# A hybrid SSD and DeltaNet step on one core: x loaded in 2 KB pieces from two queues, the first norm's sums of squares halved between two engines, two small loads held back

## The chip, the cores and the metric

The kernel runs on one core of one Trainium2 chip. The metric is the device time of one execution in microseconds (us), lower is better. Before the change it was 2331.97 us, the median of three runs (2331.62 to 2332.45).

## The reference, cut to what matters

The reference is one inference step of one layer. 336 tokens (16 learned meta tokens and 256 prompt tokens form one stream, 64 sample tokens the other) of width 2048 are normalised by their root mean square, and everything else follows from that normalised input:

```
xf = x * lax.rsqrt(jnp.mean(x * x, axis=-1, keepdims=True) + EPS)
u  = xf * norm_mix_w
z_a, xbc_a, dt_a, qkv_b, z_b, beta_b, a_b, gate_a, gate_b = split(u @ w_in)
...                              # branch A: conv, SiLU, chunked SSD scan, gated group norm
ya = ya + xs * ssd_d             # ssd_d: one number for each of 32 heads
...                              # branch B: conv, L2 norms, chunked gated delta rule
mix = sigmoid(gate_a) * (ya @ w_out[:2048]) + sigmoid(gate_b) * (ob @ w_out[2048:])
h = x + mix
h = h + square(relu(rmsnorm(h) @ w_up)) @ w_down
```

All inputs and outputs are float32. The weights w_in, w_out, w_up and w_down are large (some 340 MB are read from HBM in a run); x itself is 2.75 MB.

## The kernel before, in words

Activations are kept transposed: features on the 128 partitions, 336 tokens along the row. Each float32 product is made of three matmuls: an operand is split into a rounded high part and a low rest (`hi`, `lo` for weights, `uh`, `ul` for the normalised input), and the kernel adds hi x uh, hi x ul and lo x uh. PE is TensorE, ACT ScalarE, DVE VectorE, POOL GpSimd, and SP the engine that issues nearly all loads and stores.

**The weight stream.** Weights come in chunks `raw` of 512 KB, in a fixed order, numbered here from 0. `wload(n)` (L198) issues the load of chunk n; there are three buffers, so the load of chunk n waits until the split of chunk n - 3 has read its buffer. `wsplit(n)` writes `hi` on ACT (L61) and `lo` on DVE (L64; for chunk 3 on POOL). A projection of 256 columns (`pbig`, L58) takes four chunks, 24 matmuls each. Chunks 0 to 3 are the first projection, made while `uh` and `ul` are still being written; chunks 4 to 7 are the second.

**The start (L288 to L379).** x lies in three tiles x0, x1, x2 of 112 tokens on the partitions and 2048 features in a row. For each tile there is a sum of squares (`sumsq`, into `ssx`), a root (`root`: scale and add on DVE, power on POOL, into `rsx`), and 16 transposes on PE in four groups (`flip`, into a PSUM tile `pu`), copied to `xT`. The roots are laid on a diagonal (`spread_d`, `dgx`) and multiplied by a matrix of ones (`prx`), so that each partition holds the root of every token (`rbx`). Before the transposes PE multiplies the identity eight times (`pwarm`).

**The splits of u (L380 to L387 and the loop at L460).** `u_scale(k)` multiplies a feature block of `xT` by `rbx` (`ut`, even k on DVE, odd k on POOL); `u_split(k)` writes `uh` on ACT and `ul` on DVE. Six matmuls of the first projection follow each of the 16 blocks.

**Behind it.** Small parameters are loaded (L476 to L504) into `cra`, `crb`, `sra`, `srb`, `pb`, `wt` and `dvec`; `nega` is computed from `pb` on ACT and stands in ACT's queue between two `uh`; `wt` is split (`wtr`) and multiplied with u (`ptok`, 32 matmuls), from which per-token numbers are computed (`tok`, `la`) and summed on PE (`pcum`). `dvec` holds `ssd_d` and is first used much later. `xT` is stored to DRAM (`xTd`, L999, 16 stores) and four scratch tensors there are filled with zeros (`aD`, `uD`, L1004, 12 stores), all for later use.

**What sets the order.** PE runs in the order of the program text. Inside a `manual_schedule()` block (L342 to L472) all engines do; outside it, a scheduler with its own time estimates orders the other engines, SP's queue among them. Each DMA issued takes the next of eight completion semaphores, and waits until the DMA that had it before has landed. An engine runs its queue in order, and SP is an engine in this sense: an issue that waits holds up all behind it. The tile pool of x is given back after the last transpose (`xctx.close()`), and `cra` and its neighbours lie in that memory.

Of the kernel before, what the change touches and what calls it, by code (L numbers as in the profile page):

```python
# [8 lines left out]
F32 = mybir.dt.float32  # L9
F32R = mybir.dt.float32r  # L10
AF = mybir.ActivationFunctionType
ALU = mybir.AluOpType
# [3 lines left out]
D = 2048  # L16
KD = D // P
# [7 lines left out]
EPS = 1e-6  # L25
# [17 lines left out]
def tile_hybrid_step(ctx: ExitStack, tc: tile.TileContext, i: dict, o: dict):  # L43
    nc = tc.nc
# [9 lines left out]
    def scr(name):  # L54
        return pss.tile([P, 512], F32, tag="sc", name=name)

    def mm(out, lhsT, rhs, start=True, stop=True, **kw):
        nc.tensor.matmul(out, lhsT=lhsT, rhs=rhs, start=start, stop=stop, **kw)  # L58

    def act(out, in_, func=AF.Copy, **kw):  # L60
        nc.scalar.activation(out=out, in_=in_, func=func, **kw)  # L61

    def tt(eng, out, a, b, op):
        eng.tensor_tensor(out=out, in0=a, in1=b, op=op)  # L64
# [4 lines left out]
    V, G = nc.vector, nc.gpsimd  # L69
    MUL, ADD, SUB = ALU.mult, ALU.add, ALU.subtract  # L70
# [5 lines left out]
    ident = const.tile([P, P], F32, name="ident")  # L76
    make_identity(nc, ident)
    ones = const.tile([P, P], F32, name="ones")
# [6 lines left out]
    def transp(out, in_):  # L85
        n = in_.shape[0]
        nc.tensor.transpose(out, in_, ident[:n, :n])
# [10 lines left out]
    def new_u(name):  # L98
        return (keep.tile([P, KD, NT], F32R, tag="uh", name=name + "h"),
                keep.tile([P, KD, NT], F32R, tag="ul", name=name + "l"))  # L100

    uh, ul = new_u("u")
    acc = keep.tile([P, KD, NO], F32, name="acc")

    par = const.tile([P, 73], F32, name="par")
# [4 lines left out]
    dvec = const.tile([P, 16], F32, name="dvec")  # L110
# [82 lines left out]
    def wload(n):  # L193
        if n >= len(stream) or n in raws:
            return
        raw = wpool.tile([P, 4, 256], F32, tag="raw", name="raw", bufs=3)
        for c0, src in stream[n]:
            nc.sync.dma_start(raw[:, :, c0:c0 + src.shape[1]], src.rearrange("(k p) c -> p k c", p=P))  # L198
        raws[n] = raw

    def wsplit(n):
        if n >= len(stream) or n in split:
            return
        wload(n)
        hi = wpool.tile([P, 4, 256], F32R, tag="hi", name="hi", bufs=3)
        act(hi, raws[n])
        lo = wpool.tile([P, 4, 256], F32R, tag="lo", name="lo", bufs=3)
        tt(G if n == 3 else V, lo, raws[n], hi.bitcast(F32), SUB)
        split[n] = hi, lo
# [62 lines left out]
    sp0 = start.enter_context(tc.tile_pool(name="sp0", bufs=1))  # L272
# [3 lines left out]
    zero = sp0.tile([P, 4 * DG // P], F32, name="zero")  # L276
# [11 lines left out]
    xs = []  # L288
    segs = [[(0, "meta", 0, 16), (16, "pr", 0, 96)], [(0, "pr", 96, 112)], [(0, "pr", 208, 48), (48, "sa", 0, 64)]]
    src = {"meta": i["meta_tokens"], "pr": i["x_prompt"][0], "sa": i["x_sample"][0]}  # L290
    def load_x(n):
        for p0, s, r0, nr in segs[n]:
            nc.sync.dma_start(xs[n][p0:p0 + nr, :], src[s][r0:r0 + nr, :])

    for n in range(3):
        xs.append(xp.tile([112, D], F32, name=f"x{n}"))
    load_x(0)
    load_x(1)
    prow = sp0.tile([73, P], F32, name="prow")
    for r0, name, nr in ((NM, "norm_mix_w", 16), (SN, "ssd_norm_w", 16), (NP_, "norm_mlp_w", 16), (CB_, "ssd_conv_b", 24), (GN, "gdn_norm_w", 1)):  # L300
        nc.sync.dma_start(prow[r0:r0 + nr, :], i[name][0].rearrange("(t c) -> t c", c=P))
    load_x(2)
    warm = sp0.tile([P, 1], F32, name="warm")
    act(warm, ones[:, 0:1], AF.Square)

    def load_cols(dst, row, n):
        ps = scr("pcol")
        transp(ps[:, :n], row[:n, :])
        V.tensor_copy(dst, ps[:, :n])
# [2 lines left out]
    xT = [cpool.tile([P, 4, NT], F32, tag=t, name="xT", bufs=b) for t, b in (("q", 2), ("k", 2), ("v", 1))]  # L312
    xT.append(sp0.tile([P, 4, NT], F32, name="xT3"))
    junk = acc.rearrange("p k n -> p (k n)")[:112, :]
    ssx = sp0.tile([112, 4], F32, name="ssx")
    rsx = sp0.tile([112, 3], F32, name="rsx")
    dgx = sp0.tile([112, 3, 112], F32, name="dgx")
    rbx = sp0.tile([P, NT], F32, name="rbx")
    HD = D // 2

    def sumsq(f, x, d0, n):
        d = junk[:, d0:d0 + x.shape[1]]
        if f is act:
            act(d, x, AF.Square, accum_out=ssx[:, n:n + 1])
        else:
            V.scalar_tensor_tensor(out=d, in0=x, scalar=1.0, in1=x, op0=MUL, op1=MUL, accum_out=ssx[:, n:n + 1])

    def flip(n, k):
        ps = scr("pu").rearrange("p (k t) -> p k t", k=4)[:, :, :112]
        for m in range(4):  # L330
            transp(ps[:, m, :], xs[n][:, (k + m) * P:(k + m + 1) * P])
        return xT[k // 4][:, :, n * 112:(n + 1) * 112], ps

    def root(n):
        r = rsx[:, n:n + 1]
        V.tensor_scalar(out=r, in0=ssx[:, n:n + 1], scalar1=1.0 / D, scalar2=EPS, op0=MUL, op1=ADD)
        tt(G, r, r, nhalf_pow[:112, 0:1], ALU.pow)

    def spread_d(n):
        V.tensor_scalar(out=dgx[:, n, :], in0=ident[:112, :112], scalar1=rsx[:, n:n + 1], scalar2=None, op0=MUL)  # L340

    manual = ExitStack()  # L342
    manual.enter_context(tc.manual_schedule())

    pw_ = scr("pwarm")
    for n in range(8):
        mm(pw_[:, :P], ident, ident)
    prx = psb.tile([P, 512], F32, tag="big", name="prx")
    sumsq(act, xs[0], 0, 0)
    for k in range(0, KD, 4):  # L350
        (V.tensor_copy if k < 8 else act)(*flip(0, k))
    root(0)
    sumsq(V, xs[1], D, 1)
    for k in range(0, KD, 4):
        act(*flip(1, k))
    root(1)
    load_cols(par, prow, 73)
    for n in range(3):
        wload(n)
    sumsq(act, xs[2][:, :HD], 0, 2)  # L360
    sumsq(V, xs[2][:, HD:], D, 3)
    tt(V, ssx[:, 2:3], ssx[:, 2:3], ssx[:, 3:4], ADD)
    root(2)
    spread_d(0)
    spread_d(1)
    act(*flip(2, 0))
    late = [flip(2, k) for k in (4, 8, 12)]
    spread_d(2)
    wsplit(0)
    for n in range(3):  # L370
        mm(prx[:, n * 112:(n + 1) * 112], ones[:112, :], dgx[:, n, :])
    act(rbx, prx[:, :NT])
    for a in late:
        act(*a)
    xctx.close()
    sp = start.enter_context(tc.tile_pool(name="sp", bufs=1))
# [107 lines left out]
    srb_src = i["state_gdn_conv"][0, 0].rearrange("k (t c) -> (k t) c", c=P)  # L484
    for n in range(2):
        nc.sync.dma_start(srb[n], srb_src[n * 72:(n + 1) * 72, :])
    for h in range(2):
        nc.sync.dma_start(dvec[h * 64:(h + 1) * 64, :], i["ssd_d"][0].rearrange("(t h) -> h t", h=2)[h].partition_broadcast(64))
    pb = sp.tile([P, 2, 48], F32, name="pb")
# [16 lines left out]
    for n in range(2):  # L506
        w, wr = wt[:, n * 8:(n + 1) * 8, :], wpool.tile([P, 8, P], F32R, tag="hi", name="wtr", bufs=3)
# [697 lines left out]
    with tc.manual_schedule():  # L1205
        for t in range(3):
            final_part(7, t)
            r, n = frs[:, t:t + 1], toks[t][1]
            stt(r[n], fss[n, t, 7:8], 1.0 / D, fsum[n, t:t + 1], MUL, ADD)
            tt(G, r[n], r[n], nhalf_pow[n, 0:1], ALU.pow)  # L1210
        for m in range(2):
            for t, (_, n, t0) in enumerate(toks):
                dst = o["y_prompt"][0, t0:t0 + P, :] if t < 2 else o["y_sample"][0]
                w, r = slice(m * H, (m + 1) * H), frs[n, t:t + 1]
# [36 lines left out]
```

## Time and profile before

| | |
|---|---|
| median of three runs | 2331.97 us |
| the profiled execution, its own time | 2331.78 us |
| its span in the profile | 2330.1 us |
| PE busy | 2300.5 us, 99% of the span |
| DVE, ACT, POOL busy | 58%, 46%, 14% |
| HBM traffic | 155 GB/s over the span |
| granted TensorE clock, mean | 0.994 |

A share of busy time is an average over the whole run: in forty equal slices of some 58 us, the first and the last are the only ones in which PE is less than nine tenths busy. Times of rows are us from the start of the span.

### The profile page before, as it was taken

How to read it: one execution, taken by the hardware profiler on the slowest of the kernel's cores; microseconds unless marked ns; L12 is line 12 of the kernel's file. 1: busy time of each engine (PE TensorE's matmuls, PEld its weight loads, DVE VectorE, ACT ScalarE, POOL GpSimd, SP SyncE). 2: the span in 40 equal slices, each digit the busy share in tenths (PEclk: the TensorE clock that was granted, in tenths of full speed). 3: DMA queues.
4: the chain of work that ended last, by engine and by line, in shares of the span. 5: the costliest groups of instructions: out<-in, count | busy, mean ns of one | idle time of the engine just before them, and what ended most of it. 6: DMA issues, size and time to landing. Idle time of an engine off the chain costs nothing.

```text
span 2330.1 us, 40632 instructions
## 1 busy us (share of the span) xinstructions
PE 2300.5 (99%) x16393; PEld 2278.1 (98%) x16393; DVE 1360.9 (58%) x2147; ACT 1064.6 (46%) x1830; POOL 333.0 (14%) x488
## 2 busy tenths in 40 slices
PE   7999999999999999999999999999999999999997
PEld 7999999999999999999999999999999999999997
DVE  6674858585865547658668467444444444444444
ACT  5655546455445545554554445433343244324433
POOL 3151505041211102212212110000000000000000
PEclk8999999999999999999999999999999999999999
DMA  7846555545575555555546644544554444445543
GB/s 194 225 121 188 143 159 150 159 135 173 156 200 170 148 164 139 154 150 144 156 148 165 170 142 145 154 149 151 148 154 149 150 148 151 154 146 153 168 141 117
DMA packets 411046, 362.87 MB, mean 156 GB/s; under 512 B 48329, under 2 KB 407834, under 8 KB 410394
## 3 DMA queue, kind: packets, MB, share of 16 engines
q1 hardware_dynamic: 410746, 360.15, 53.1%
q8 instruction: 128, 2.10, 0.4%
q14 instruction: 60, 0.49, 0.1%
q10 hardware_dynamic: 112, 0.13, 0.0%
HBM read 340.57 MB, written 19.66 MB: 155 GB/s over the span
## 4 chain that ended last, share of the span: by engine, by line
PE 91%; DVE 5%; DMA 2%; issue 1%; SPq 1%; ACT 0%; ACTq 0%; POOL 0%; DVEq 0%
PE pbig L58 84%; DVE lo L64 1%; PE po L58 1%; DMA em<-rowd 1%; DVE pr L64 1%; DVE ubt L858 1%; PE pS L58 0%; PE pw L58 0%; PE pyd L58 0%; DVE c L67 0%; PE pkk L58 0%; PE pqk L58 0%; PE ph L58 0%; DMA x<-in_x_sample_dram 0%; PE pyo L58 0%
## 5 line engine op out<-in xcount | busy, mean ns | idle before, releaser
L64 DVE TENSOR_TENSOR lo<-raw,hi 128x1024 fp32r<-128x1024 f32 x591 | 739.1, 1251 | 697.3 <-ACT hi L61 688.0
L61 ACT ACTIVATE hi<-raw 128x1024 fp32r<-128x1024 f32 x592 | 626.3, 1058 | 892.1 <-PE pbig L58 834.6
L58 PE MATMUL pbig<-uh,hi 128*128 128x320 f32 (+2 forms) x2176 | 688.9, 317 | 3.1 <-ACT uh L61 3.1
L58 PE MATMUL pbig<-ul,hi 128*128 128x320 f32 (+2 forms) x2176 | 681.9, 313 | 2.9 <-DVE ul L67 2.7
L58 PE MATMUL pbig<-uh,lo 128*128 128x320 f32 (+2 forms) x2176 | 680.8, 313 | 1.6 <-DVE lo L64 1.6
L58 PEld LDWEIGHTS pbig<-uh,hi 128*128 128x128 f32 x2176 | 410.9, 189 | 9.1 <-ACT uh L61 3.8
L58 PEld LDWEIGHTS pbig<-ul,hi 128*128 128x128 f32 x2176 | 410.8, 189 | 4.7 <-DVE ul L67 4.3
L58 PEld LDWEIGHTS pbig<-uh,lo 128*128 128x128 f32 x2176 | 411.0, 189 | 2.4 <-DVE lo L64 2.4
L58 PE MATMUL pbig<-hh,hi 128*128 128x320 f32 x1024 | 318.0, 311 | 0.0
L58 PE MATMUL pbig<-hnl,hi 128*128 128x320 f32 x1024 | 317.1, 310 | 0.0
L58 PE MATMUL pbig<-hl,hi 128*128 128x320 f32 x1024 | 316.3, 309 | 0.0
L58 PE MATMUL pbig<-hh,lo 128*128 128x320 f32 x1024 | 316.2, 309 | 0.0
L58 PE MATMUL pbig<-hnh,lo 128*128 128x320 f32 x1024 | 315.8, 308 | 0.0
L58 PE MATMUL pbig<-hnh,hi 128*128 128x320 f32 x1024 | 315.1, 308 | 0.0
L58 PEld LDWEIGHTS pbig<-hnh,lo 128*128 128x128 f32 x1024 | 192.9, 188 | 0.0
L58 PEld LDWEIGHTS pbig<-hl,hi 128*128 128x128 f32 x1024 | 192.6, 188 | 0.0
L58 PEld LDWEIGHTS pbig<-hh,hi 128*128 128x128 f32 x1024 | 192.6, 188 | 0.0
L58 PEld LDWEIGHTS pbig<-hnh,hi 128*128 128x128 f32 x1024 | 192.4, 188 | 0.2
L58 PEld LDWEIGHTS pbig<-hh,lo 128*128 128x128 f32 x1024 | 192.5, 188 | 0.0
L58 PEld LDWEIGHTS pbig<-hnl,hi 128*128 128x128 f32 x1024 | 192.2, 188 | 0.0
L58 PE MATMUL pbig<-yh,hi 128*128 128x320 f32 x512 | 161.1, 315 | 0.0
L58 PE MATMUL pbig<-yh,lo 128*128 128x320 f32 x512 | 157.5, 308 | 0.0
(303 smaller groups left out, 2425.8 us busy)
## 6 DMA issues: line engine op xcount, KB each, us to landing
raw<-in_w_in_dram SPq DMA_DIRECT2D x256, 512.0 KB, 3.8
raw<-in_w_up_dram SPq DMA_DIRECT2D x128, 512.0 KB, 3.8
raw<-in_w_down_dram SPq DMA_DIRECT2D x128, 512.0 KB, 3.4
raw<-in_w_out_dram SPq DMA_DIRECT2D x64, 512.0 KB, 3.4
raw<-in_w_in_dram SPq DMA_DIRECT2D x32, 256.0 KB, 3.1
em<-rowd SPq DMA_DIRECT2D x8, 512.0 KB
u<-uD SPq DMA_DIRECT2D x4, 768.0 KB, 7.1
eab<-rowd SPq DMA_DIRECT2D x8, 336.0 KB, 6.9
```

What stands on the lines that cost most here:

```text
L58: nc.tensor.matmul(out, lhsT=lhsT, rhs=rhs, start=start, stop=stop, **kw)
L61: nc.scalar.activation(out=out, in_=in_, func=func, **kw)
L64: eng.tensor_tensor(out=out, in0=a, in1=b, op=op)
L858: V.tensor_reduce(out=ubt[:NE, j0:, s], in_=v, axis=AX.X, op=ADD)
```

## The change

The load of x is cut into pieces of 512 features (2 KB a row). The order is x0, x2, x1; x0 and x2 are issued from SP's queue, x1 from ACT's. The five loads of `prow` come behind all of x. For each of the three tiles the sum of squares is made in two halves of 1024 features, the first on ACT, the second on DVE (`sums`), and added (`rooted`). The root of each tile is spread by its own `prx` matmul as soon as it stands in PE's order (`spread`), instead of three at the end. Copies of transposes are dealt between DVE and ACT, `load_cols(par, ...)` moves behind the last `spread`, `pwarm` has 14 products instead of eight. At last, two one-column DVE instructions write `dvec` and `zero` from the last block of `uh`, always to zero, so that the two loads of `dvec` and the zero fills cannot start before that block is there.

```diff
-    def load_x(n):
-        for p0, s, r0, nr in segs[n]:
-            nc.sync.dma_start(xs[n][p0:p0 + nr, :], src[s][r0:r0 + nr, :])
...
-    load_x(0)
-    load_x(1)
+    start_order = ExitStack()
+    start_order.enter_context(tc.manual_schedule())
+    for n in (0, 2, 1):
+        for q in range(4):
+            w = slice(q * D // 4, (q + 1) * D // 4)
+            for p0, s, r0, nr in segs[n]:
+                (nc.scalar if n == 1 else nc.sync).dma_start(xs[n][p0:p0 + nr, w], src[s][r0:r0 + nr, w])
     prow = sp0.tile([73, P], F32, name="prow")
...
-    load_x(2)
+    start_order.close()
...
+    def sums(n, m):
+        sumsq((act, V)[m], xs[n][:, m * HD:(m + 1) * HD], m * HD, 2 * n + m)
+    def rooted(n):
+        tt(V, rsx[:, n:n + 1], ssx[:, 2 * n:2 * n + 1], ssx[:, 2 * n + 1:2 * n + 2], ADD)
+        r = rsx[:, n:n + 1]
+        V.tensor_scalar(out=r, in0=r, scalar1=1.0 / D, scalar2=EPS, op0=MUL, op1=ADD)
+        tt(G, r, r, nhalf_pow[:112, 0:1], ALU.pow)
+    def spread(n):
+        mm(prx[:, n * 112:(n + 1) * 112], ones[:112, :], dgx[:, n, :])
...
-    for n in range(8):
+    for n in range(14):
         mm(pw_[:, :P], ident, ident)
...
-    sumsq(act, xs[0], 0, 0)
...
+    sums(0, 0)
+    cp(*f0[0])
+    sums(0, 1)
+    rooted(0)
...
+    spread_d(2)
+    spread(2)
+    load_cols(par, prow, 73)
+    act(*f2[0])
     wsplit(0)
...
+    for t in (dvec, zero):
+        V.tensor_scalar(out=t[:, 0:1], in0=uh[:, KD - 1, 0:1].bitcast(F32), scalar1=0.0, scalar2=0.0, op0=ALU.min, op1=ALU.max)
     for h in range(2):
         nc.sync.dma_start(dvec[h * 64:(h + 1) * 64, :], i["ssd_d"][0].rearrange("(t h) -> h t", h=2)[h].partition_broadcast(64))
```

SP's queue at the start, before the change: from the last load of x to the small parameters.

```order
L293 DMA x_147<-in_x_prompt_dram 48x2048
L293 DMA x_147<-in_x_sample_dram 64x2048
L198 DMA raw<-in_w_in_dram 128x4x256 x3
L488 DMA dvec<-in_ssd_d_dram 64x16x1
L476 DMA cra<-in_ssd_conv_w_dram 96x128
L198 DMA raw<-in_w_in_dram 128x4x256
L480 DMA crb_473<-in_gdn_conv_w_dram 96x128
```

The same place of SP's queue after the change, from the last pieces of x on.

```order
L299 DMA x_147<-in_x_prompt_dram 48x512
L299 DMA x_147<-in_x_sample_dram 64x512
L302 DMA prow<-in_norm_mix_w_dram 16x128
L302 DMA prow<-in_ssd_norm_w_dram 16x128
L302 DMA prow<-in_norm_mlp_w_dram 16x128
L302 DMA prow<-in_ssd_conv_b_dram 24x128
L302 DMA prow<-in_gdn_norm_w_dram 1x128
L198 DMA raw<-in_w_in_dram 128x4x256 x3
L1024 DMA xTd<-xT 128x320 x2
L498 DMA cra<-in_ssd_conv_w_dram 96x128
L502 DMA crb_501<-in_gdn_conv_w_dram 96x128
```

The loads of `prow` now stand between x and the first weights, `dvec` has left the place behind the weights, and two stores of `xTd` have come there.

SP's queue later, before the change: from the loads of `wt` to the loads of chunk 7 and 8 (the first `raw` behind the `aD` fills is chunk 7).

```order
L503 DMA wt<-in_w_in_dram 128x16x32
L198 DMA raw<-in_w_in_dram 128x4x256
L504 DMA wt<-in_w_in_dram 128x16x32
L198 DMA raw<-in_w_in_dram 128x4x256
L999 DMA xTd<-xT 128x320 x12
L999 DMA xTd<-xT_164 128x320 x4
L1004 DMA aD_107<-zero 128x516 x3
L198 DMA raw<-in_w_in_dram 128x4x256
```

The same place after the change; the last `raw` is again chunk 7.

```order
L528 DMA wt<-in_w_in_dram 128x16x32
L198 DMA raw<-in_w_in_dram 128x4x256
L529 DMA wt<-in_w_in_dram 128x16x32
L198 DMA raw<-in_w_in_dram 128x4x256
L1024 DMA xTd<-xT 128x320
L513 DMA dvec<-in_ssd_d_dram 64x16x1 x2
L1024 DMA xTd<-xT 128x320 x9
L1024 DMA xTd<-xT_182 128x320 x4
L1029 DMA aD_107<-zero 128x516 x3
L198 DMA raw<-in_w_in_dram 128x4x256
```

Both loads of `dvec` now stand here, one behind the other, with 13 stores of `xTd`, three fills and then chunk 7 behind them.

DVE's queue at the start, before the change: from the sum of squares of x1 to the first `ut`.

```order
L326 SCALAR_TENSOR_TENSOR acc,ssx<-x_146 112x2048
L336 TENSOR_SCALAR rsx<-ssx 112x1
L309 COPY par<-pcol 128x73
L326 SCALAR_TENSOR_TENSOR acc,ssx<-x_147 112x1024
L64 TENSOR_TENSOR ssx<-ssx 112x1
L336 TENSOR_SCALAR rsx<-ssx 112x1
L340 TENSOR_SCALAR dgx<-ident,rsx 112x112 x3
L64 TENSOR_TENSOR lo<-raw,hi 128x1024
L64 TENSOR_TENSOR ut<-xT,rbx 128x336 x2
```

The same place after the change, from the copy of a group of x1 on.

```order
L378 COPY xT<-pu 128x4x112
L326 SCALAR_TENSOR_TENSOR acc,ssx_186<-x_147 112x1024
L64 TENSOR_TENSOR rsx<-ssx_186 112x1
L346 TENSOR_SCALAR rsx<-rsx 112x1
L335 TENSOR_SCALAR dgx<-ident,rsx 112x112
L386 COPY xT<-pu 128x4x112
L335 TENSOR_SCALAR dgx<-ident,rsx 112x112
L310 COPY par<-pcol 128x73
L64 TENSOR_TENSOR lo<-raw,hi 128x1024
L64 TENSOR_TENSOR ut<-xT,rbx 128x336 x2
```

DVE has four copies and three half sums instead of two copies, one whole sum and one half, and the copy of `par`, which waits for PE's last work on x, now stands ahead of the first `lo`.

## Rows read from the trace of the kernel before

**Rows 1.** The page: busy time by engine, and the chain that ended last by engine.

```profile
PE 2300.5 (99%) x16393; PEld 2278.1 (98%) x16393; DVE 1360.9 (58%) x2147; ACT 1064.6 (46%) x1830; POOL 333.0 (14%) x488
...
PE 91%; DVE 5%; DMA 2%; issue 1%; SPq 1%; ACT 0%; ACTq 0%; POOL 0%; DVEq 0%
```

**Rows 2.** The view of waits, engine PE alone, from 50 us to the end, its largest class: total us, times, longest us.

```profile
PE pbig L58 <- DVE lo L64: 1.6, 3, 0.7
```

**Rows 3.** The timeline of the start: start us, duration us, engine, line, operation, count, and in brackets the idle time before it and what ended that.

```profile
1.58 3.78 PE L58 MATMUL pwarm<-ident 128*128 128x128 f32 x16 [1.58 <-POOL ident masks.py:199]
...
8.03 1.37 DVE L351 COPY xT<-pu 128x448 f32<-128x448 f32 x2 [8.03 <-PE pu L87]
...
14.99 1.23 DVE L326 SCALAR_TENSOR_TENSOR acc<-x 112x1024 f32<-112x1024 f32 x1 [2.28 <-DMA x<-in_x_sample_dram]
...
16.33 0.16 DVE L64 TENSOR_TENSOR ssx<-ssx 112x1 f32<-112x1 f32 x1
...
16.53 0.15 DVE L336 TENSOR_SCALAR rsx<-ssx 112x1 f32<-112x1 f32 x1
...
17.34 0.28 DVE L340 TENSOR_SCALAR dgx<-ident,rsx 112x112 f32<-112x112 f32 x1 [0.29 <-POOL rsx L64]
17.57 1.23 DVE L64 TENSOR_TENSOR lo<-raw,hi 128x1024 fp32r<-128x1024 f32 x1
...
18.04 1.49 PE L58 MATMUL prx<-dgx,ones 112*128 112x112 f32 x6
...
19.57 0.45 ACT L61 ACTIVATE rbx<-prx 128x336 f32<-128x336 f32 x1 [2.03 <-PE prx L58]
...
20.05 1.62 DVE L64 TENSOR_TENSOR ut<-xT,rbx 128x336 f32<-128x336 f32 x2 [1.26 <-ACT rbx L61]
```

**Rows 4.** The view by windows: stretch, its length, busy us of each engine with the count, granted clock, DMA share, GB/s.

```profile
20.05:39.16 19.11, 14.40 (x67) 12.99 (x68) 18.96 (x22) 10.02 (x18) 13.23 (x9) 0.77 0.28 71
41.58:43.59 2.01, 2.00 (x7) 1.89 (x8) 2.01 (x5) 1.36 (x3) 0.00 (x0) 0.50 1.19 293
...
45.00:50.00 5.00, 3.92 (x27) 3.74 (x26) 2.98 (x10) 3.00 (x6) 0.95 (x4) 0.97 1.03 356
```

**Rows 5.** The timeline from 40 to 49 us, columns as in rows 3.

```profile
40.84 0.24 ACT L61 ACTIVATE nega<-pb 128x48 f32<-128x48 f32 x1 [7.39 <-DMA pb<-in_gdn_a_log_dram]
...
41.58 2.01 DVE L67 SCALAR_TENSOR_TENSOR ul<-ut,par,uh 128x336 fp32r<-128x336 f32 x4 [2.42 <-ACT uh L61]
...
41.59 0.65 PE L58 MATMUL pbig<-uh,hi 128*128 128x336 f32 x1 [0.76 <-ACT uh L61]
...
45.99 1.15 ACT L61 ACTIVATE wtr<-wt 128x512 fp32r<-128x512 f32 x2 [3.04 <-DMA wt<-in_w_in_dram]
...
48.17 0.30 PE L87 MATMUL pcol<-ident,crb 96*128 96x96 f32 x1 [1.08 <-DVE cwa L309]
...
48.39 0.40 PE L58 MATMUL ptok<-uh,wtr 128*128 128x336 f32 x1
```

**Rows 6.** The timeline of SP's queue: start us, duration of the issue us.

```profile
11.60 0.69 SPq L488 DMA_DIRECT2D dvec<-in_ssd_d_dram  x1
...
26.45 0.61 SPq L488 DMA_DIRECT2D dvec<-in_ssd_d_dram  x1
...
28.28 0.39 SPq L198 DMA_DIRECT2D raw<-in_w_in_dram  x1
28.71 6.12 SPq L491 DMA_DIRECT2D pb<-in_gdn_dt_bias_dram  x1
...
43.35 8.30 SPq L999 DMA_DIRECT2D xTd<-xT  x16
51.69 1.45 SPq L1004 DMA_DIRECT2D aD<-zero  x3
53.88 0.38 SPq L198 DMA_DIRECT2D raw<-in_w_in_dram  x1
```

**Rows 7.** The view of the tile dvec: its two loads from issue to landing, us.

```profile
DMA to landing us min/median/max: 12.0/13.4/14.8
```

**Rows 8.** The view of DMA traffic: one row each for 29 to 36 us, 18 to 19 us, 15 to 18 us and 52 to 55 us.

```profile
DMA packets 747, 0.01 MB, mean 1 GB/s; under 512 B 741, under 2 KB 747, under 8 KB 747
...
DMA packets 586, 0.21 MB, mean 206 GB/s; under 512 B 386, under 2 KB 586, under 8 KB 586
...
DMA packets 1053, 1.05 MB, mean 349 GB/s; under 512 B 32, under 2 KB 1053, under 8 KB 1053
...
DMA packets 825, 1.19 MB, mean 396 GB/s; under 512 B 92, under 2 KB 515, under 8 KB 824
```

**Rows 9.** The timeline of ACT and DVE around the split of chunk 7, and pieces of the chain that ended last (start us, us, what).

```profile
58.98 1.06 ACT L61 ACTIVATE hi<-raw 128x1024 fp32r<-128x1024 f32 x1 [1.94 <-DVE c L67]
...
60.08 1.22 DVE L64 TENSOR_TENSOR lo<-raw,hi 128x1024 fp32r<-128x1024 f32 x1
...
71.49 0.30 DVE L64 TENSOR_TENSOR la<-pl,nega 128x144 f32<-128x144 f32 x1
...
53.57 1.86 PE pbig L58 x12
...
55.77 17.06 PE pbig L58 x111
72.83 0.56 PE pcum L58 x6
```

More of the change, by code (lines that the diff above doesn't have):

```diff
@@ L314, in tile_hybrid_step @@
     junk = acc.rearrange("p k n -> p (k n)")[:112, :]
-    ssx = sp0.tile([112, 4], F32, name="ssx")
     rsx = sp0.tile([112, 3], F32, name="rsx")
@@ L332, in flip @@
         return xT[k // 4][:, :, n * 112:(n + 1) * 112], ps
[L334 to L337, printed above, removed]
     def spread_d(n):
         V.tensor_scalar(out=dgx[:, n, :], in0=ident[:112, :112], scalar1=rsx[:, n:n + 1], scalar2=None, op0=MUL)
+    ssx = sp0.tile([112, 6], F32, name="ssx6")
+    def sums(n, m):
[7 more added lines that the diff above has]
+        mm(prx[:, n * 112:(n + 1) * 112], ones[:112, :], dgx[:, n, :])
     manual = ExitStack()
@@ L345, in tile_hybrid_step @@
     pw_ = scr("pwarm")
-    for n in range(8):
+    for n in range(14):
         mm(pw_[:, :P], ident, ident)
     prx = psb.tile([P, 512], F32, tag="big", name="prx")
-    sumsq(act, xs[0], 0, 0)
[L350 to L357, printed above, removed]
     for n in range(3):
         wload(n)
[L360 to L363, printed above, removed]
-    spread_d(0)
+    cp = V.tensor_copy
+    f0 = [flip(0, k) for k in (0, 4, 8, 12)]
+    sums(0, 0)
+    cp(*f0[0])
+    sums(0, 1)
+    rooted(0)
+    act(*f0[1])
+    f1 = [flip(1, k) for k in (0, 4)]
+    sums(1, 0)
+    sums(1, 1)
+    cp(*f0[2])
+    act(*f0[3])
+    f1 += [flip(1, k) for k in (8, 12)]
+    spread_d(0)
+    spread(0)
+    rooted(1)
+    sums(2, 0)
+    cp(*f1[0])
+    f2 = [flip(2, 0)]
+    sums(2, 1)
+    rooted(2)
+    act(*f1[1])
+    f2.append(flip(2, 4))
     spread_d(1)
-    act(*flip(2, 0))
-    late = [flip(2, k) for k in (4, 8, 12)]
+    spread(1)
+    cp(*f1[2])
+    act(*f1[3])
+    f2 += [flip(2, k) for k in (8, 12)]
     spread_d(2)
+    spread(2)
+    load_cols(par, prow, 73)
+    act(*f2[0])
     wsplit(0)
-    for n in range(3):
-        mm(prx[:, n * 112:(n + 1) * 112], ones[:112, :], dgx[:, n, :])
     act(rbx, prx[:, :NT])
-    for a in late:
+    for a in f2[1:]:
         act(*a)
```

## The prediction

> **What bounds the kernel now.** First I read the busy times of the page: PE is busy for 99% of the span and makes 91% of the chain that ended last [rows 1]. Then PE's waits from 50 us on: the largest class is 1.6 us in all [rows 2]. So from 50 us to the end PE runs one list of matmuls without a pause; whatever reaches PE's list earlier or later by some us moves the end by as much, unless a new wait appears behind it. All that can be gained lies before 50 us, and the timeline shows it in three pieces. The norm of x ends at the first `ut`, 20.05 us [rows 3]. Then DVE is the bound: 18.96 us busy of 19.11 until 39.16 [rows 4]. Then a tail of waits: ACT stood 7.39 us before `nega` for a load of `pb`, so the last four `ul` of DVE came 2.42 us late; `wtr` waited 3.04 us for `wt`; the first `ptok` matmul ran at 48.39 [rows 5]. SP's queue says why `pb` and `wt` were late: an issue behind each load of `dvec` did not get through, one for 6.12 us [rows 6], and each `dvec` took 12.0 to 14.8 us from issue to landing for 4 KB [rows 7].
>
> **The change part by part.**
>
> *The norm.* DVE has four copies of transposes (1.37/2 = 0.69 each), three half sums (1.23), three adds and three scales (0.16 + 0.15) and three diagonals (0.28) [rows 3]: 2.7 + 3.7 + 0.9 + 0.8 = 8.2 us. They begin after the first group of x0 is flipped, and PE comes to that behind 14 `pwarm` products. Eight took 3.78 us from 1.58 [rows 3]; 14 end at 8.2 at the same pace, at about 7 if the six new ones run at the faster level. With half a us to a whole one for the flip, DVE starts at 7.6 to 9 (8.03 before) and is through at 15.8 to 17.2. The halves of x2 needed here: 2.75 MB take 7.9 us at the 349 GB/s at which 1 KB weight rows moved [rows 8]; 16 issues on SP at 0.38 to 0.69 us [rows 6] make 6 to 11 us. I take 12.5 us as the landing; DVE comes to that sum at about 13, so it is hidden; if x2 lands at 15 it costs 2 us. Behind the last diagonal come one `prx` (two of the six matmuls of 1.49, so 0.5), the transpose and copy of `par` (0.4, a new link: `lo` stands behind it) and `lo` of chunk 0 (1.23) [rows 3]: first `ut` at 18 to 19.3 instead of 20.05. I take 1.2 us earlier, bounds -2 (x2 late) and +2.
>
> *The splits of u.* Same instructions, DVE-bound: 19.11 us from first `ut`, then the last four `ul`, 2.01 us [rows 4]. `pb` and `wt` no longer stand behind a `dvec`, so `nega` does not wait: last `ul` at 20.05 - 1.2 + 19.11 + 2.01 = 40.0 instead of 43.6. PE gains less. It was only 0.76 us idle for that wait [rows 5], since it was behind: its granted clock was 0.50, the 1.2 GHz level [rows 4], and 0.97 in 45 to 50 us. Without the 0.76 us pause I estimate that it is back at 2.4 GHz some 3 us earlier, so that ten matmuls take 0.154 us (17.06/111 [rows 9]) instead of 0.28 (2.00/7 [rows 4]), 1.2 us less; then the 1.08 us wait before the last `pcol` [rows 5] goes too, since `wt` has landed. Together 0.76 + 1.2 + 1.08 = 3.0, with the norm 4.2 us: `ptok` at 44.2 instead of 48.39. Bounds: 3 (the clock stays low) to 6 (it never falls).
>
> *The two loads of `dvec`.* They now wait for the last block of u and are issued at 40.1, one behind the other, and 13 stores of `xTd`, three fills and the load of chunk 7 stand behind them on SP, as the order shows. What does a `dvec` load cost? In 29 to 36 us nothing else moved: 741 packets of under 512 B in 7 us, 106 a us, at 1 GB/s, though chunk 4 had been issued at 28.28 [rows 6, 8]. The load is 64 rows of 16 elements with a stride, 1024 elements; at 106 a us, 9.7 us, which fits the 12.0 us to landing with some 2 us of latency [rows 7]. Two in a row: the second lands at 40.1 + 12.0 + 9.7 = 61.8. The lower bound is that they run side by side, 40.1 + 12.0 to 14.8 = 52 to 55; the upper bound is two full landings one after the other, 40.1 + 29.6 = 69.7. I take the middle one, since 106 a us was the rate of the whole queue.
>
> *What is late next.* With eight semaphores, the eighth DMA behind a `dvec` waits for it to land: seven `xTd` are issued ahead, six `xTd` (8.30/16 = 0.52 us each) and three fills (1.45) behind [rows 6], 4.6 us, so chunk 7 is issued at 66.4. The bytes ahead of it, 13 x 160 KB and 3 x 258 KB, and its own 512 KB are 3.5 MB, 8.7 us at 396 GB/s [rows 8]: it lands at about 70.3. `hi` (1.06) and `lo` (1.22) [rows 9] end at 72.6. Before, this `lo` ended at 61.30, with PE reaching chunk 7 at 65.0 (12 + 111 matmuls of 24 a chunk put `pcum` three matmuls into chunk 9, and 51 x 0.154 before 72.83 is 65.0 [rows 9]). So the gain of 4.2 us brings PE to chunk 7 at 60.8, and there it stands for some 10 us. Behind that `lo` DVE does the per-token numbers without much idle time, until `la` at 71.79, and PE's `pcum` came 1.0 us behind that [rows 9]. The same 10.5 us from 72.6 give `la` at 83.1 and `pcum` at 83.1 instead of 72.83: 10.3 us late. If PE's clock falls in the pause, that hides inside DVE's 10.5 us. After `pcum` DVE has slack again and PE goes on as before. The lead of the norm is inside this sum, since it moves the issue of `dvec`; that of the tail is lost.
>
> *At nothing:* the zero fills (needed much later), the two one-column instructions, the loads of `prow` (`par` is copied last), the four issues on ACT (done by 3 us, before x is there).
>
> The sum on the profiled execution: 2331.78 + 10.3 = 2342.1, say 2342 us. That execution lies 0.2 us under the median of the runs, so nothing is to be corrected.
>
> **The rivals.**
>
> *No stall.* The `dvec` loads are cheap, as their bytes suggest, and the gain at `ptok` holds to the end: 2331.78 - 4.2 = 2327.6. It decides when chunk 7's `lo` ends before PE gets there, so the second `dvec` must land by about 47 (`lo` ends 4.6 + 3.9 + 2.3 us later, and may end at 58 at the latest for `pcum` to stay in place); from a landing at 51.5 on the change loses. For: in 18 to 19 us 386 packets under 512 B passed in one us [rows 8], so the engines can be faster than 106 a us. Against: they were waiting ready behind the weights then, and the rest of that load needed until 26.4 (11.60 + 14.8). [...]
>
> *Side by side.* Both `dvec` loads land at 52 to 55. Then chunk 7 is issued at 57 to 60, its `lo` ends at 63 to 66, `la` at 73.5 to 76.5, and `pcum` is 0.7 to 3.7 us late: 2332.5 to 2335.5, say 2334. For: nothing in the trace shows two of them in the queue at once. Against: the rate was the same near 106 with the queue otherwise empty, so a limit that both share is likelier.
>
> *x starves the start.* With eight semaphores over both queues, SP's third pieces wait for ACT's first, and x2 lands at 15 or later; then the norm ends 1 to 2 us later than before, everything down to `dvec` with it, and the stall stands on top: 2331.78 + 10.3 + 1.2 + 2 = 2345.3. For: small pieces, in-order waits. Against: 1 KB rows moved at 349 GB/s [rows 8]. The Trainium skill (DMA: Bandwidth & Descriptors, Rules for kernel authors) holds that transfers under 64 KB pay mostly overhead and that full bandwidth wants 1 MiB or more, by which pieces of 32 to 224 KB would be slow and this rival would hold; no run here shows such pieces of x yet.
>
> **How the numbers follow.** Forecast 57%, side by side 18%, no stall 19%, starved start 6%. The predicted time is the forecast's, 2342. Its own range, from the spread of landing (58 to 64) and of the norm, is 2338 to 2346. For 8 in 10 I need the side-by-side case and part of the no-stall one: 2329 to 2346. About 0.2%, 4.7 us, is what a measurement of this kernel can tell from no change. Slower by more: nearly all of the forecast and the starved start, 0.59; within: side by side, the lower end of the forecast and the smaller half of no stall, 0.28; faster by more: the rest of no stall (up to 6 us of gain), 0.13.
>
> **What would show it.** Right: first `ut` at 18 to 19.3 us; no wait before `nega` or `wtr`; `ptok` at 43 to 46; `dvec` issued near 40 with 20 us or more to the second landing, some 100 packets a us and almost no GB/s beside it; PE idle for about 10 us near 61, released by ACT `hi` or DVE `lo`, and ACT waiting for a `raw` load there. Wrong: chunk 7 in place before PE asks, weights moving while `dvec` is in flight, or a first `ut` later than 20 us.

## The result, and the profile after

The changed kernel takes 2346.15 us, the median of four runs (2345.44 to 2347.32), beside 2332.21 us for the kernel before in the same measurement (2331.62 to 2332.91). The ratio is 1.006, with a 95% interval of 1.0048 to 1.0073. The profiled execution took 2345.44 us, its span is 2343.7 us, 13.6 more than before. The forecast was 2342 with a range of 2329 to 2346: the direction and the place are right, the size is 4 us short, and the time lies 0.15 us beyond the range.

The page of the changed kernel: busy time by engine, and the chain that ended last by engine.

```profile
PE 2300.4 (98%) x16405; PEld 2278.4 (97%) x16405; DVE 1361.6 (58%) x2155; ACT 1063.4 (45%) x1830; POOL 334.9 (14%) x488
...
PE 92%; DVE 3%; DMA 2%; SPq 1%; issue 0%; ACT 0%; POOL 0%; ACTq 0%; DVEq 0%; POOLq 0%
```

PE does the same work in the same time [rows 1]; all that is new is time in which it stands. The view of waits, PE from 50 us on (total us, times, longest), says where.

```profile
PE pbig L58 <- ACT hi L61: 12.0, 1, 12.0
PE pcum L58 <- DVE la L64: 1.4, 1, 1.4
PE pbig L58 <- DVE lo L64: 1.3, 2, 1.0
```

One wait of 12.0 us, for the high part of a weight chunk, where the largest class before was 1.6 us in all [rows 2]. SP's queue (start us, duration of the issues us) shows why that chunk was late.

```profile
42.55 1.41 SPq L513 DMA_DIRECT2D dvec<-in_ssd_d_dram  x2
44.01 23.62 SPq L1024 DMA_DIRECT2D xTd<-xT  x13
67.73 1.39 SPq L1029 DMA_DIRECT2D aD<-zero  x3
69.22 0.40 SPq L198 DMA_DIRECT2D raw<-in_w_in_dram  x1
```

The 13 stores behind the two `dvec` loads took 23.62 us to issue; 16 took 8.30 before [rows 6]. Chunk 7 was issued at 69.22 instead of 53.88. In the meantime almost nothing moved. The view of DMA traffic for 44 to 62 us, where seven stores of 160 KB had been issued:

```profile
DMA packets 1928, 0.01 MB, mean 0 GB/s; under 512 B 1928, under 2 KB 1928, under 8 KB 1928
## 3 DMA queue, kind: packets, MB, share of 16 engines
q1 hardware_dynamic: 1928, 0.01, 4.7%
```

1928 packets in 18 us are 107 a us, the rate of [rows 8], and the engines' recorded share is only 4.7%. The timeline of ACT and DVE around chunk 7:

```profile
74.68 1.06 ACT L61 ACTIVATE hi<-raw 128x1024 fp32r<-128x1024 f32 x1 [19.35 <-DMA raw<-in_w_in_dram]
...
75.77 1.22 DVE L64 TENSOR_TENSOR lo<-raw,hi 128x1024 fp32r<-128x1024 f32 x1 [17.33 <-ACT hi L61]
...
87.21 0.30 DVE L64 TENSOR_TENSOR la<-pl,nega 128x144 f32<-128x144 f32 x1
```

And two pieces of the chain that ended last, the load of chunk 7 and the first product that hangs on DVE's per-token numbers:

```profile
69.22 5.36 DMA raw<-in_w_in_dram
...
87.56 0.79 PE pcum L58 x6
```

In the chain `pcum` came at 87.56 instead of 72.83 [rows 9], 14.73 us later; the span grew by 13.6, so about 1 us was regained behind it.

### The profile page after: what moved, and what is told of

It is laid out like the page before. It is cut to its first block, busy times and chain, and to the rows that moved or that the text cites. A ratio compares the mean times of both kernels' runs of the same rounds, so it can differ in the third digit from the quotient of the medians.

```text
span 2343.7 us, 40697 instructions
## 1 busy us (share of the span) xinstructions
PE 2300.4 (98%) x16405; PEld 2278.4 (97%) x16405; DVE 1361.6 (58%) x2155; ACT 1063.4 (45%) x1830; POOL 334.9 (14%) x488
## 4 chain that ended last, share of the span: by engine, by line
PE 92%; DVE 3%; DMA 2%; SPq 1%; issue 0%; ACT 0%; POOL 0%; ACTq 0%; DVEq 0%; POOLq 0%
PE pbig L58 86%; DVE lo L64 1%; PE po L58 1%; DMA raw<-in_w_in_dram 1%; DMA xTd<-xT 1%; PE pS L58 0%; PE pw L58 0%; SPq L1024 0%; PE pyd L58 0%; PE ph L58 0%; PE pkk L58 0%; PE pqk L58 0%; DVE c L67 0%; PE pyo L58 0%; PE pks L58 0%
```

## The experiments

All times are medians beside the kernel before on the same chip (2332.08 to 2332.62 us in these runs); ratios are to that, with 95% intervals. Names of tiles are those of the change.

### Is it the two loads, and is it the hold?

The first four runs take the suspects apart. `e2_rows_gated` keeps the whole change, but loads `ssd_d` as whole rows and deals them out on POOL, held back to the same point:

```diff
-    for t in (dvec, zero):
+    drow = sp.tile([P, 32], F32, name="drow")
+    for t in (drow, zero):
...
+    nc.sync.dma_start(drow, i["ssd_d"][0].partition_broadcast(P))
     for h in range(2):
-        nc.sync.dma_start(dvec[h * 64:(h + 1) * 64, :], i["ssd_d"][0].rearrange("(t h) -> h t", h=2)[h].partition_broadcast(64))
+        G.tensor_copy(dvec[h * 64:(h + 1) * 64, :], drow[h * 64:(h + 1) * 64, :].rearrange("p (t h) -> p h t", h=2)[:, h, :])
```

> The changed kernel, but ssd_d is loaded as 128 contiguous rows of 32 numbers and dealt to dvec by two small POOL copies; the hold on this load and on the zero fills stays. Theory (the element-wise pair of dvec loads blocks SP's queue and so delays chunk 7): no pause of PE at chunk 7, what is left is ptok 1.7 us earlier than before (46.66 against 48.39), so about 2330.3 us. Rival (something else of the change, such as the held fills or the stores of xTd, delays chunk 7): still 2340 to 2346 us.

Measured: 2329.8 us, ratio 0.9989 (0.998 to 0.9999). SP's queue no longer stands behind the load:

```profile
43.17 0.34 SPq L513 DMA_DIRECT2D drow<-in_ssd_d_dram  x1
43.55 8.70 SPq L1026 DMA_DIRECT2D xTd<-xT  x13
52.35 1.39 SPq L1031 DMA_DIRECT2D aD<-zero  x3
54.34 3.92 SPq L198 DMA_DIRECT2D raw<-in_w_in_dram  x5
```

The same 13 stores take 8.70 us, and PE has no wait over 1.0 us from 50 us on. The form of the load, with its place, makes the whole loss.

`e7_before_gate` is the kernel before with nothing but the hold:

```diff
+    for t in (dvec, zero):
+        V.tensor_scalar(out=t[:, 0:1], in0=uh[:, KD - 1, 0:1].bitcast(F32), scalar1=0.0, scalar2=0.0, op0=ALU.min, op1=ALU.max)
```

> The kernel before with the two holding DVE instructions of the change alone: x is loaded and normed as before. Theory (the hold makes nearly all of the loss, the new start only moves the issue of dvec): dvec is issued near 41.3 instead of 42.6, PE pauses some 12 us at chunk 7, 2344 to 2345 us. Rival (the new start makes the loss): 2331 to 2333 us.

Measured: 2345.4 us, ratio 1.0057 (1.0042 to 1.0072): two one-column instructions of DVE cost 13.3 us, nearly all of the change. The waits of PE from 50 us on, and SP's queue:

```profile
PE pbig L58 <- ACT hi L61: 12.6, 1, 12.6
```

```profile
41.38 1.42 SPq L490 DMA_DIRECT2D dvec<-in_ssd_d_dram  x2
42.84 23.57 SPq L1001 DMA_DIRECT2D xTd<-xT  x13
```

`e3_one_dvec` is the changed kernel with one of the two loads, and asks whether they run side by side:

```diff
+    G.memset(dvec[64:, :], 0.0)
-    for h in range(2):
+    for h in range(1):
```

> The changed kernel with only one of the two element-wise loads of dvec; the other half of dvec is zero, so the ssd_d term of every other head is left out. Theory (106 elements a us, one load behind the other): the queue is free 9.7 us earlier, about 2336 to 2337 us, and PE's pause at chunk 7 falls from 12.0 to about 2.5 us. Rival (the two loads run side by side, and the price is the latency): no change, 2345 to 2346 us.

Measured: 2338.01 us, ratio 1.0026 (1.0016 to 1.0036), 8.1 us under the changed kernel. PE's wait for `hi` is 4.6 us, and the stores behind one load take 14.79 us instead of 23.62:

```profile
42.86 0.70 SPq L514 DMA_DIRECT2D dvec<-in_ssd_d_dram  x1
43.60 14.79 SPq L1025 DMA_DIRECT2D xTd<-xT  x13
```

So the second load costs 8.8 us of its own: 1024 elements at 107 a us are 9.6 us. The two run one after the other; in the trace of the changed kernel they land at 55.11 and 63.68. The wait was longer than the 2.5 us expected.

`e6_act_queue` issues the two loads from ACT's queue, to see whether it is SP's queue or the element-wise load that blocks:

```diff
-        nc.sync.dma_start(dvec[h * 64:(h + 1) * 64, :], ...
+        nc.scalar.dma_start(dvec[h * 64:(h + 1) * 64, :], ...
```

> The changed kernel with the two element-wise loads of dvec issued from ACT's queue instead of SP's, still held by the last block of u. Theory A (what is blocked is the queue that the load stands in): weights and xTd flow on SP's queue beside it, no pause at chunk 7, 2330 to 2332 us (ACT gives some 1.4 us for the two issues). Theory B (element-wise loads occupy all sixteen DMA engines, whatever the queue): chunk 7 is as late as in the changed kernel, 2343 to 2347 us.

Measured: 2346.88 us, ratio 1.0061 (1.0047 to 1.0075), no better. The view of DMA traffic for 45 to 62 us, where q10 is ACT's queue and q1 SP's:

```profile
DMA packets 2154, 0.39 MB, mean 23 GB/s; under 512 B 1861, under 2 KB 2153, under 8 KB 2153
...
q1 hardware_dynamic: 328, 0.37, 6.0%
q10 hardware_dynamic: 1825, 0.01, 4.7%
```

SP's stores got 23 GB/s beside the loads of the other queue, where they moved at 355 GB/s in the changed kernel from 65 to 70 us. Two stores issued at 42.63 and 43.07, as the loads began, landed only at 54.18 and 61.49; one issued at 63.93, when the loads were through, landed at 66.41. The Trainium skill (DMA: Bandwidth & Descriptors, Issuing engines are not separate DMA queues) says that DMAs issued by different engines run on the same engines and interleave; the slow stores agree. But SP's queue stood for a second reason as well. Its row for the stores, and two pieces of the chain up to chunk 7's `lo`:

```profile
38.30 27.43 SPq L1024 DMA_DIRECT2D xTd<-xT  x14
```

```profile
43.06 20.85 DMA dvec<-in_ssd_d_dram
...
63.93 0.32 SPq L1024
```

SP issued no store from 43.83 to 55.03, just behind the landing of the first `dvec` (55.02), and after two more none until 63.93, just behind that of the second (63.91). Each time it took the completion semaphore that this load had held, although the load was on the other queue. So a second queue is no way past here; but the run doesn't separate theory B from the semaphores, and how late chunk 7 would be by the shared DMA engines alone is not shown.

`e4_before_rows` puts the cheap load into the kernel before, at its old place, with nothing else of the change (the diff of `e2_rows_gated` without the hold).

> The kernel before with nothing changed but the loads of dvec, replaced by contiguous rows and two POOL copies. Theory (the stalls behind dvec also made pb and wt late before the change): nega and wtr no longer wait for loads, ptok at about 45.3 instead of 48.39, 2329 us. Rival (these waits were hidden by PE's own lag): 2331.5 to 2332.5 us.

Measured: 2327.4 us, ratio 0.9978 (0.9968 to 0.9987), the fastest of all, 4.7 us under the kernel before and 18.8 under the changed one. `ptok` starts at 44.53. The Trainium skill (DMA: Bandwidth & Descriptors, Rules for kernel authors) says that a strided last dimension becomes one descriptor for each element and is to be rearranged so that it is contiguous; the 4-byte packets above and this run bear it out.

### Why is the new start late?

With the cheap load in both, the new start with its hold loses 2.4 us to the old one (2329.8 against 2327.4 in the same measurement; ten executions each, 2328.07 to 2332.78 and 2326.44 to 2329.24), and the first `ut` comes at 22.09 instead of 19.36. Eight runs, all built on `e2_rows_gated`, took it apart. The starts (us) of four instructions in the timeline, and the times (`ut` is DVE's first; POOL's own can begin before it):

| run | first sum of x0 | first `ut` | `ptok` | `pcum` | median | ratio (interval) |
|---|---|---|---|---|---|---|
| kernel before | 6.96 | 20.05 | 48.39 | 72.66 | | |
| changed kernel | 9.29 | 21.47 | 46.66 | 87.56 | 2346.15 | 1.006 (1.0048 to 1.0073) |
| `e4_before_rows` | 7.11 | 19.36 | 44.53 | 68.81 | 2327.4 | 0.9978 (0.9968 to 0.9987) |
| `e2_rows_gated` | 9.39 | 22.09 | 47.29 | 72.42 | 2329.8 | 0.9989 (0.998 to 0.9999) |
| `e8_raw_first` | 9.38 | 23.15 | 46.64 | 71.08 | 2329.3 | 0.9988 (0.9979 to 0.9997) |
| `e9_whole_rows` | 10.45 | 21.19 | 46.39 | 70.70 | 2329.53 | 0.9989 (0.998 to 0.9998) |
| `e10_whole_raw` | 10.33 | 22.60 | 45.54 | 71.08 | 2329.55 | 0.9988 (0.9979 to 0.9997) |
| `e11_one_queue` | 5.11 | 20.97 | 46.17 | 71.23 | 2329.19 | 0.9989 (0.998 to 0.9998) |
| `e12_one_queue_whole` | 6.98 | 21.35 | 46.50 | 71.12 | 2330.27 | 0.9992 (0.9983 to 1.0001) |
| `e13_prow_act` | 7.07 | 21.64 | 46.85 | 72.48 | 2331.28 | 0.9994 (0.9985 to 1.0004) |
| `e14_par_early` | 6.97 | 20.68 | 45.90 | 74.26 | 2335.27 | 1.0013 (1.0004 to 1.0022) |
| `e15_par_prx` | 6.93 | 19.43 | 43.34 | 72.20 | 2334.81 | 1.0014 (1.0005 to 1.0023) |

Each row is one trace, and small differences say little: with the same new start the first `ut` came at 21.26 to 22.09 (the changed kernel, `e2_rows_gated`, `e3_one_dvec`, `e6_act_queue`), with the old one at 19.36 to 20.26 (the kernel before, `e4_before_rows`, `e7_before_gate`).

First the loads. `e8_raw_first` puts the first three weight loads ahead of `prow`, `e9_whole_rows` loads x in whole rows (`range(1)` for `range(4)`), `e10_whole_raw` does both:

```diff
+    for n in range(3):
+        wload(n)
     prow = sp0.tile([73, P], F32, name="prow")
...
-    for n in range(3):
-        wload(n)
     cp = V.tensor_copy
```

> The kernel with contiguous rows for ssd_d and the new start (2329.8 us), with the first three weight loads moved ahead of the five loads of prow. Theory (the start is late since hi of chunk 0 waits for its load, issued behind prow): hi 2 us earlier, first ut about 1 us earlier (par's copy becomes the bound), 2328.5 to 2329 us. Rival (the norm's own chain on DVE is the bound): first ut and time as they were, 2329.8 us.

> The kernel with contiguous rows for ssd_d and the new start (2329.8 us), but x loaded in whole rows of 8 KB: five loads from the same two queues in the same order of tiles instead of 20 pieces. Theory (20 issues and the wait for one of eight semaphores make x and the weights late, not the bytes): x2 and the first weights land 2 to 3 us earlier, 2327 to 2328 us. Rival (small pieces let the norm begin earlier, which is worth more): 2330 to 2332 us.

> Both: x in whole rows from two queues and the first three weight loads ahead of prow, with contiguous rows for ssd_d. Theory: as whole rows alone or up to 0.5 us better, 2327 to 2328 us, since the weights no longer come late there. Rival (weights in flight take bandwidth from x2 and prow): 0.5 to 1 us worse than whole rows alone.

Measured: none can be told from `e2_rows_gated` in time. In `e8_raw_first` `hi` of chunk 0 came 2.5 us earlier as said (17.33 for 19.86), but `prow` was then late, and `par`'s copy at 21.67 held the first `ut` back. In `e9_whole_rows` the first sum of x0 started even later, so the number of pieces is not what makes it late.

Then the queues. `e11_one_queue` sends all pieces through SP, `e12_one_queue_whole` the five whole rows, `e13_prow_act` moves `prow` to ACT's queue besides:

```diff
-    for n in (0, 2, 1):
+    for n in (0, 1, 2):
...
-                (nc.scalar if n == 1 else nc.sync).dma_start(xs[n][p0:p0 + nr, w], src[s][r0:r0 + nr, w])
+                nc.sync.dma_start(xs[n][p0:p0 + nr, w], src[s][r0:r0 + nr, w])
```

> e2_rows_gated with all pieces of x on SP's queue, in the order x0, x1, x2. Theory A: the start is late because x1 on ACT's queue takes bandwidth from x0. Then the first sum of x0 starts near 8 us instead of 9.39, the first ut at 20.5 instead of 22.1, and the time is 2328.2. Theory B: it is late because the weights and the rows of prow stand behind all of x. Then the first sum may start earlier, but the first ut stays at 22 us or goes later, since 20 issues on one queue put prow and the weights back further: 2329.8 to 2330.5.

> e9_whole_rows with the five whole-row loads of x all on SP's queue, in the order x0, x1, x2; prow and the weights still behind. Theory A (sharing): the first sum of x0 starts near 7 us instead of 10.45, the first ut near 20, 2327.5. Theory B (prow and the weights behind x): the first sum starts near 7, but the first ut stays at 21 or later, 2329.5.

> e12_one_queue_whole with the five loads of prow on ACT's queue, so that they start at once and the weights follow x directly on SP. Theory A (sharing): as e12, 2327.5. Theory B (prow and the weights behind x): hi of chunk 0 and the copy of par are no longer late, the first ut comes at 19 to 19.5 as in the kernel before or a little earlier, and the time is that of e4_before_rows or a little less, 2327.

Measured: the first half of theory A holds. With one queue the first sum starts at 6.98 instead of 10.45 (whole rows) and at 5.11 instead of 9.39 (pieces): x1 on ACT's queue held x0 back. But the first `ut` hardly followed, 21.35 and 20.97, which is nearer to theory B. In `e13_prow_act` theory B in its turn wants 19 to 19.5, and the first `ut` stayed at 21.64, though `hi` of chunk 0 ran at 17.54. Neither theory gives that. DVE's timeline in `e12_one_queue_whole`:

```profile
17.26 0.28 DVE L335 TENSOR_SCALAR dgx<-ident,rsx 112x112 f32<-112x112 f32 x1
20.07 0.23 DVE L310 COPY par<-pcol 128x73 f32<-128x73 f32 x1 [2.53 <-PE pcol L87]
20.22 1.22 DVE L64 TENSOR_TENSOR lo<-raw,hi 128x1024 fp32r<-128x1024 f32 x1
21.35 2.31 DVE L64 TENSOR_TENSOR ut<-xT,rbx 128x336 f32<-128x336 f32 x2
```

The last diagonal stands at 17.26, as early as before (17.34 [rows 3]). Then DVE waits 2.53 us for `par`, and `lo` of chunk 0, which ran beside `prx` before (17.57), runs only after it. `e14_par_early` moves `load_cols(par, prow, 73)` ahead of the last transposes; `e15_par_prx` also moves the last `prx` ahead of the last eight transposes:

```diff
     rooted(2)
+    load_cols(par, prow, 73)
     act(*f1[1])
...
-    f2 += [flip(2, k) for k in (8, 12)]
     spread_d(2)
     spread(2)
-    load_cols(par, prow, 73)
+    f2 += [flip(2, k) for k in (8, 12)]
```

> e12_one_queue_whole with the transpose and copy of par (the line load_cols) moved ahead of the last transposes of x. There x, prow and the weights arrive as early as in the kernel before, and still the first ut came at 21.35: DVE stood 2.53 us before the copy of par and made lo of chunk 0 only then. Theory C (the place of par puts lo on the path): lo runs at 18.3 to 19.6 while PE works, the first ut comes right behind rbx, at 20.3 to 20.5, and ptok at 45.5. Theory D (the transposes of x2 ahead of the last prx hold rbx, and lo is hidden anyway): the first ut stays at 21 or later. The time moves by 1 us at most, 2329 us.

> e14_par_early, and the last prx ahead of the last eight transposes of x2. If both links cost, the last prx runs at 17.8 instead of 19.27, rbx at 18.4, and lo of chunk 0 (18.3 to 19.6) ends last: first ut at 19.6, 1.7 us earlier than in e12_one_queue_whole, ptok at 44.8, and 2328.5 us. If only the place of par costs, as e14_par_early.

Measured at the first `ut`: 20.68 and 19.43. Counted from the start of the last diagonal (17.26, 17.67 and 17.78) it comes 4.09 us later in `e12_one_queue_whole`, 3.01 in `e14_par_early` and 1.65 in `e15_par_prx`. So theory C holds at this place, and both links cost: 1.1 us the place of `par`, 1.4 that of the last `prx`. DVE in `e14_par_early`, where `lo` is hidden again and `rbx` comes last:

```profile
17.67 0.27 DVE L335 TENSOR_SCALAR dgx<-ident,rsx 112x112 f32<-112x112 f32 x1
18.17 1.23 DVE L64 TENSOR_TENSOR lo<-raw,hi 128x1024 fp32r<-128x1024 f32 x1 [0.23 <-ACT hi L61]
20.68 1.62 DVE L64 TENSOR_TENSOR ut<-xT,rbx 128x336 f32<-128x336 f32 x2 [1.29 <-ACT rbx L61]
```

DVE in `e15_par_prx`:

```profile
17.78 0.27 DVE L335 TENSOR_SCALAR dgx<-ident,rsx 112x112 f32<-112x112 f32 x1
18.28 1.23 DVE L64 TENSOR_TENSOR lo<-raw,hi 128x1024 fp32r<-128x1024 f32 x1 [0.23 <-ACT hi L61]
19.43 1.62 DVE L64 TENSOR_TENSOR ut<-xT,rbx 128x336 f32<-128x336 f32 x2
```

But the times went the other way, to 2335.27 and 2334.81 us, where 2329 and 2328.5 were expected, though `ptok` came 3.2 us earlier in `e15_par_prx` than in `e12_one_queue_whole`. PE's longest wait from 50 us on in `e15_par_prx`, and two windows (length, busy us of PE, PEld, DVE, ACT, POOL, granted clock, DMA share, GB/s):

```profile
PE pcum L58 <- DVE la L64: 4.4, 1, 4.4
```

```profile
70.00:75.00 5.00, 2.80 (x14) 2.80 (x15) 3.65 (x10) 2.10 (x4) 1.44 (x2) 0.53 0.93 256
75.00:80.00 5.00, 5.00 (x20) 5.00 (x20) 0.66 (x3) 0.56 (x3) 0.00 (x0) 0.50 0.32 101
```

PE now reached `pcum` before DVE had made `la`, and stood 4.4 us there; the granted clock fell meanwhile to 0.50, the 1.2 GHz level, where it is 1.00 in both windows of `e12_one_queue_whole`. The scheduler had also dealt DVE's work behind `ptok` in another order: three more `c` (0.48 us each) and one more `lo` now stand between the last `tok` and `la`, DVE waits 2.54 us for a `hi` there, and `la` starts at 71.85 instead of 70.77. Of the 5.2 us by which this span is longer, 1.1 stand at `pcum` (72.20 against 71.12) and the other 4.1 come behind it, which fits a stretch of some 8 us at half the clock (it is 0.86 from 80 to 82 us). `e14_par_early` has the same wait, 3.9 us, and 0.50 from 75 to 82 us. That a fixed order of DVE there would keep the gain was not tried, nor was the changed kernel with the old load and no hold.

## Why the prediction was wrong in size

- **What bounds the kernel.** Right: PE's list is unchanged [rows 1], and one wait before it makes the loss.
- **The norm, the step that failed.** "I take 1.2 us earlier": DVE's first `ut` came 1.42 us later, 2.6 us off, and 2.45 us of the 4.4 by which the sum is short come from it. That lies within the 2 us either way that the step allowed, but the upper end of the range did not carry it on top of the late landing. Two waits were missing in the sum. DVE stood 2.74 us for the second half of x0, where the sum had a wait for x2 alone, and its last diagonal ended at 17.77 instead of 15.8 to 17.2; `e11_one_queue` shows that x1 beside it held x0 back. And the weights were issued at 15.15 instead of 10.05, behind 16 pieces of x and `prow`, whose loads I had set at nothing because `par` is copied last: DVE stood 1.45 us before `lo` of chunk 0. The copy of `par` ended at 18.87, before `hi`, and cost no more here than the 0.4 us counted; it is the next link, as `e12_one_queue_whole` shows, where the weights come in time. The timeline of the changed kernel's start (columns as in rows 3):

```profile
9.29 1.06 ACT L61 ACTIVATE acc<-x 112x1024 f32<-112x1024 f32 x1 [5.11 <-DMA x<-in_x_prompt_dram]
...
10.81 1.22 DVE L326 SCALAR_TENSOR_TENSOR acc<-x 112x1024 f32<-112x1024 f32 x1 [2.74 <-DMA x<-in_x_prompt_dram]
...
15.15 1.51 SPq L198 DMA_DIRECT2D raw<-in_w_in_dram  x3
...
17.49 0.28 DVE L335 TENSOR_SCALAR dgx<-ident,rsx 112x112 f32<-112x112 f32 x1
...
18.15 0.39 PE L58 MATMUL prx<-dgx,ones 112*128 112x112 f32 x2
...
18.64 0.23 DVE L310 COPY par<-pcol 128x73 f32<-128x73 f32 x1 [0.87 <-PE pcol L87]
19.24 1.06 ACT L61 ACTIVATE hi<-raw 128x1024 fp32r<-128x1024 f32 x1 [3.20 <-DMA raw<-in_w_in_dram]
...
20.20 0.43 ACT L61 ACTIVATE rbx<-prx 128x336 f32<-128x336 f32 x1
...
20.32 1.23 DVE L64 TENSOR_TENSOR lo<-raw,hi 128x1024 fp32r<-128x1024 f32 x1 [1.45 <-ACT hi L61]
...
21.47 2.32 DVE L64 TENSOR_TENSOR ut<-xT,rbx 128x336 f32<-128x336 f32 x2
```

  The last `prx` is through at 18.54, 1 us earlier than before (18.04 + 1.49 = 19.53 [rows 3]): that much of the norm's gain was real. ACT then stands for chunk 0 (3.20 us), `rbx` and `lo` behind it. The rival of the starved start, with its late first `ut`, gave 2345.3 and came nearest, but not by its mechanism, x late by its pieces and their semaphores: in `e9_whole_rows` x is five loads, fewer than the eight semaphores, and its first sum came later still (10.45).
- **The splits of u.** Right: from the first `ut` to the end of the last `ul` (42.46) are 21.0 us, as the 19.11 + 2.01 forecast. The tail gained 3.15 us (`ptok` 1.73 earlier although the norm was 1.42 later), forecast 3.0.
- **The two `dvec` loads.** Right in size: issued at 42.55 instead of 40.1, late by the norm; the second landed at 63.68, 21.1 us behind the issue of the pair, where 12.0 + 9.7 = 21.7 were forecast. From the issue of the pair to that of chunk 7 are 26.7 us, forecast 26.3.
- **The landing of chunk 7.** Too short: 5.36 us instead of 3.9. I had taken 396 GB/s; the windows of the changed kernel show 355 and 277, and the clock in the pause:

```profile
65.00:70.00 5.00, 0.00 (x0) 0.00 (x0) 0.00 (x0) 0.00 (x0) 0.00 (x0) 0.74 0.98 355
70.00:75.00 5.00, 0.00 (x0) 0.00 (x0) 0.00 (x0) 0.32 (x1) 0.00 (x0) 0.50 1.01 277
75.00:80.00 5.00, 3.88 (x12) 3.46 (x13) 3.97 (x9) 4.34 (x8) 0.00 (x0) 0.50 1.10 294
```

- **What hides behind it.** Right: from the end of that `lo` (76.99) to the end of `la` (87.51) are 10.5 us, as forecast, and the low clock until 80 us is hidden beside it, since `pcum` still waited 1.4 us for `la`.
- **The sum.** 10.3 forecast, 14.73 at `pcum`: 2.45 for the later issue of the loads, 0.4 to chunk 7's issue, 1.5 for its landing, 0.1 for the rest. About 1 us came back later, which I had not counted.

The rival without a stall fell (the pause is there), and so did the one side by side: `e3_one_dvec` shows 8.8 us for the second load alone.

## What to carry to other kernels

Price a small load by its packets, not its bytes, and look at what stands behind it in the queue, at what must wait for its semaphore, and at who else uses the DMA engines; if it is element-wise, load whole rows and deal them out on an idle engine. A hold that moves a load "to where it is needed" also moves it in front of whatever is due there. At the start, gaining on one engine is worth nothing until the last of all inputs of the next step (here weights, `par` and the roots) is earlier too, and a gain that is handed on can still be lost at the next wait.

## What was not expected of the hardware

- That 4-byte packets hold up what stands behind them in their queue was forecast; that they hold up large stores of another queue as well was not: two of 160 KB took 11.6 and 18.4 us to land beside them, one took 2.5 us after them (`e6_act_queue`). And the recorded share of the DMA engines was below 11% then (4.7 + 6.0 + 0.1). A low busy share of DMA is no sign that a queue is free.
- Loading two tiles from two queues delays the first: with whole rows x0 was ready at 10.45 us with x1 on the other queue, at 6.98 with all on one.
- A wait of 4.4 us of PE cost 4.1 us more behind it, by the granted clock of 0.50 that followed (`e15_par_prx`), while behind the 12.0 us pause of the changed kernel the low clock cost nothing, since PE still waited 1.4 us for `la` there.
